# A different order of matmuls and loads in the first phase of a one-core transformer-layer kernel

## The chip, the cores and the metric

The kernel runs on one core of a Trainium2 chip. TensorE does the matmuls, VectorE (DVE in the profile) and ScalarE (ACT) the elementwise work, GpSimd (POOL) a little of it, and SyncE (SP) issues nearly all loads from HBM. The metric is the device time of one execution in microseconds; lower is better.

## The reference

One layer over 256 latent tokens `x` and 256 context tokens `ctx`, each 2048 wide, in float32. What the first phase computes is this part:

```python
mod   = silu(c) @ w_mod + b_mod          # one row of 6*2048; sa, ca, ga, sm, cm, gm are its six pieces
mod_c = silu(c_ctx) @ w_mod + b_mod      # the same for the context's conditioning vector
h_c = rmsnorm(ctx, w) * (1 + ca_c) + sa_c
h   = rmsnorm(x,   w) * (1 + ca)   + sa
k_c = rmsnorm(split(h_c @ w_k));  q, k = rope(rmsnorm(split(h @ w_q))), rope(rmsnorm(split(h @ w_k)))
```

After it come the values, the rest of the queries and keys, attention, a pooling mixer, gates, an output projection and a squared-ReLU MLP. A change in the first phase leaves all of these as they are.

## The kernel before, in words

Every product of float32 operands is made of three matmuls: each operand is split in a high part (rounded) and a low part (the remainder), and high·high, low·high and high·low are added up in PSUM (`mm3`). A weight chunk of 128x1024 (512 KB) is loaded to a `raw` buffer by SP; ACT copies it rounded to a `whi` tile and DVE subtracts to get `wlo` (in `load_next`, the lines 232 and 233). The order of all loads is written down ahead of time: `plan(...)` appends to the list `stream`, and `wchunk` takes the next chunk, after `load_next` has issued the loads up to `ahead` chunks further on. SP issues in the order of that list and waits at a load whose buffer isn't free yet.

The contraction over the 2048 model channels is cut in 16 tiles of 128 channels. The first phase loops over these tiles, `f` = 0 to 15. For each one:

- `mod_tile(f)` uses four `w_m` chunks (2 MB) in 32 small matmuls (the `mod` tile in the profile) to get shift and scale of that tile's channels, for latents and context at once. `mod_columns` turns the result into columns with four tiny matmuls (`modT`) and a few short ACT and DVE instructions.
- `hidden(f, 0)` and `hidden(f, 1)` make the modulated, normalised latents (`hL`) and context tokens (`hC`) of the tile: two DVE instructions and one ACT instruction each. They need the factor `rms`, which comes from sums of squares over all channels (`ssq`); for the context that sum is made by `context_squares` from the four `cT` loads.
- The first halves of keys and queries (512 of 1024 columns) are accumulated tile by tile: `kx` (keys of latents), `q` (queries of latents), `kc` (keys of context), six matmuls of 128x512 each. The weights come in pairs of tiles: chunk `j` of `w_k` and of `w_q` holds the tiles 2j and 2j+1.

All matmuls of this phase stay in the order in which the program gives them (`ordered_pe`); ACT's and DVE's instructions are put in an order by the compiler's scheduler. Products are taken from one chain (`order`, `side`) at a pace written in a table: `PACE[f]` half-products are done around `mod_columns`, so tile 0's keys are first multiplied at `f` = 2, and the chain then trails the modulation by about two tiles. The two chunks of the last pair are multiplied after the loop, with the rest of the chain.

Buffers matter for the order. The `raw` tag has five buffers of 512 KB; the `w_m` chunks of even tiles and all `w_k`, `w_q` chunks use them. The `w_m` chunks of odd tiles use other memory (`mod_raw`, lines 179 to 187). An even tile and one pair of `w_k` and `w_q` thus are six chunks for five buffers. In the kernel before, the pair is loaded behind the odd tile (`f` = 1, 3, 7, 9, ...), except for the third, which comes right behind tile 6:

```python
j = 2 if f == 6 else -1 if f == 5 or f % 2 == 0 else f // 2
```

The high and low parts of `w_k` lie in a tile `first` with room for two chunks, those of `w_q` in the common `whi` and `wlo` tiles. SP's load is in the lines 115 (`w_k`, `w_q` and all later weights) and 212 (`w_m`). The next phase begins with the values, `v_group(0)`, whose matmuls are on the lines 426, 427 and 429; the profile gives line 67 for every matmul that is kept in program order.

Beside all this a background generator (`late_gen`) loads the remaining pieces of `w_mod` and sums them on DVE (line 606), at a rate tied to the weight chunks loaded. It starts after the first phase; chunks loaded earlier give it no step.

Of the kernel before, what the change touches and what calls it, by code (L numbers as in the profile page):

```python
# [19 lines left out]
KT = D // P  # L20
# [28 lines left out]
def layer(ctx: ExitStack, tc, a, out):  # L49
# [21 lines left out]
    def bank(name):  # L71
        return psum.tile([P, 512], F32, tag="ps", name=name)

    def work(name, shape=None, dt=F32):
        return pool.tile(shape or [P, 512], dt, tag="w2", name=name, bufs=9)

    def s16(name, shape, dt=F32):
        return pool.tile(shape, dt, tag="s16", name=name, bufs=7)
# [4 lines left out]
    def small(name, n):  # L83
        return pool.tile([P, 16], F32, tag="sm", name=name, bufs=12)[:, 0:n]
# [14 lines left out]
    def tick():  # L99
        for w in waiting:  # L100
            w[0] -= 1
        while waiting:
            due = [w for w in waiting if w[0] <= 0]
            if not due:
                break
            waiting.remove(due[0])
            due[0][1]()
# [10 lines left out]
    def chain(*gens):  # L118
        for g in gens:
            yield from g  # L120
# [5 lines left out]
    def plan(name, *idx, rate=0.0):  # L126
        stream.append(((name,) + idx, rate))
# [3 lines left out]
    for f in range(KT):  # L131
        for i in range(4):
            plan("w_m", f, i)
            if f in (2, 3) and i % 2 == 1:
                plan("cT", 2 * f - 4 + i // 2)
            if (f, i) == (9, 0):
                plan("prq")
        j = 2 if f == 6 else -1 if f == 5 or f % 2 == 0 else f // 2
        if j >= 0:
            plan("w_k", 0, j)  # L140
            plan("w_q", 0, j)
    for n, g, rate in (("w_v", 0, 1.5), ("w_q", 1, 1.0), ("w_k", 1, 1.5), ("w_v", 1, 1.5)):
        for ch in range(8):
            plan(n, g, ch, rate=rate)
# [27 lines left out]
    FIRST_AHEAD = 3  # L172
# [69 lines left out]
    def wchunk(*key, ahead=AHEAD):  # L242
        while len(loaded) < min(done[0] + 1 + ahead, len(stream)) or loaded[done[0]][1] is None:
            if loaded and done[0] < len(loaded) and loaded[done[0]][1] is None:
                done[0] += 1
                continue
            load_next()
        got, hi, lo = loaded[done[0]]
        assert got == key, (got, key)
        loaded[done[0]] = None  # L250
        done[0] += 1
        tick()
        return hi, lo
# [5 lines left out]
    def mm3(o, l_hi, l_lo, r_hi, r_lo, start, stop):  # L259
        pe.matmul(o, l_hi, r_hi, start=start, stop=False)  # L260
        pe.matmul(o, l_hi, r_lo, start=False, stop=False)
        pe.matmul(o, l_lo, r_hi, start=False, stop=stop)

    def rsq(v, n, div, tag=None):

        mk = (lambda nm: small(nm, n)) if n <= 16 else (lambda nm: work(nm, [P, n]))
        y = mk(tag or "rq_y")
        pin(act.activation(y, v, AF.Ln, scale=div * 2.0 ** -64, bias=epsb))
        act.activation(y, y, AF.Exp, scale=-0.5, bias=ebias)
        t = mk("rq_t")  # L270
        vec.scalar_tensor_tensor(t, y, -0.5 * div, y, ALU.mult, ALU.mult)
        vec.scalar_tensor_tensor(t, v, EPS / div, t, ALU.add, ALU.mult)
        vec.scalar_tensor_tensor(y, t, 1.5, y, ALU.add, ALU.mult)
        return y
# [6 lines left out]
    cT = s16("cT", [P, KT, T])  # L281
# [3 lines left out]
    def pr(name):  # L285
        lo, hi = PRM[name]
        return prm[:, lo:hi]
# [70 lines left out]
    def tok(tiles, k, part, t):  # L358
        return tiles[k // 8][:, part, k % 8, t * P:t * P + P]

    def mod_tile(f, ps):

        raws = [wchunk("w_m", f, i, ahead=FIRST_AHEAD)[0] for i in range(4)]
        c = (f % 2) * T
        for i in range(4):
            for j in range(4):
                k = 4 * i + j  # L370
                pe.matmul(ps[32 * j:32 * j + 32, c:c + T], cv[:, k, :], raws[i][:, j * T:j * T + T],
                          start=k < 4, stop=k >= 12)
        rows = work("rows", [P, T])
        act.copy(rows, ps[:, c:c + T])
        return rows

    def mod_columns(f, rows):

        pt = bank("modT")
        for a in range(2):  # L380
            pe.matmul(pt[:, 2 * a:2 * a + 2], rows[:, a * P:a * P + P], quads, start=a == 0, stop=a == 1,
                      skip_group_check=True)
        col = small("col", 4)
        act.copy(col, pt[:, 0:4])
        c3 = col.rearrange("p (a c) -> p a c", a=2)
        vec.tensor_add(c3, c3, bias2[:, :, f:f + 1].broadcast_to([P, 2, 2]))
        vec.tensor_scalar(c3[:, 0, :], c3[:, 0, :], pr("nw")[:, f:f + 1], None, ALU.mult)
        return c3

    def hidden(f, t, c3):  # L390

        src, h = ((xT, hL), (cT, hC))[t]
        u = work("hw", [P, T])
        ht, k8 = h[f // 8], f % 8
        bias = c3[:, 1, t:t + 1]
        vec.scalar_tensor_tensor(u, src[:, f, :], c3[:, 0, t:t + 1], rms[t], ALU.mult, ALU.mult)
        act.activation(ht[:, 0, k8, :], u, AF.Identity, bias=bias)
        vec.scalar_tensor_tensor(ht[:, 1, k8, :], u, bias, ht[:, 0, k8, :].bitcast(F32), ALU.add, ALU.subtract)

    def tokens(nt):  # L400
        return [(hL, 0), (hL, 1), (hC, 0), (hC, 1)][:nt]

    def xmm(banks, toks, k, hi, lo, sl, first, last):
        for ps, (h, t) in zip(banks, toks):
            mm3(ps, tok(h, k, 0, t), tok(h, k, 1, t), hi[:, sl], lo[:, sl], first, last)
# [72 lines left out]
    fb = {}  # L478
    held = {}

    def pair_steps(n, j):

        w = "w_q" if n == "q" else "w_k"
        if w not in fb:
            fb[w] = [bank(f"{w}_{t}") for t in range(4 if n != "q" else 2)]
        hi, lo = held[w, j]
        for kk in range(2):
            k = 2 * j + kk
            for t in range(2):
                t4 = t + (2 if n == "kc" else 0)  # L490
                xmm([fb[w][t4]], [tokens(4)[t4]], k, hi, lo, slice(kk * 512, kk * 512 + 512), k == 0, k == KT - 1)
                yield

    def steps(n):
        for _ in range(n):
            next(side, None)

    order = [("kx", 0), ("q", 0), ("kx", 1), ("q", 1), ("kc", 0), ("kc", 1), ("kx", 2), ("q", 2), ("kc", 2)]
    for j in range(3, 7):
        order += [("kx", j), ("q", j), ("kc", j)]  # L500
    side = chain(*(pair_steps(*o) for o in order))
    PACE = (0, 0, 4, 4, 6, 6, 8, 8) + (6,) * 8

    cols = {}
    total = []

    def context_squares(i):

        sq = [work("sq") for _ in range(2)]
        for h in range(2):  # L510
            act.activation(sq[h], cT[:, 4 * i + 2 * h:4 * i + 2 * h + 2, :].rearrange("p a t -> p (a t)"), AF.Square)
        vec.tensor_add(sq[0], sq[0], sq[1])
        if total:
            vec.tensor_add(total[0], total[0], sq[0])
        else:
            total.append(sq[0])


    context = {4: (0, 1), 5: (2, 3, 4), 6: (5, 6)}
    ordered_pe[0] = True  # L520
    sb = bank("ssq")
    for i in range(4):
# [2 lines left out]
    for f in range(KT):  # L525
        if f % 2 == 0:
            ps = bank("mod")
        rows = mod_tile(f, ps)
        if f == 4:
            sq = total[0]  # L530
            vec.tensor_add(sq[:, 0:T], sq[:, 0:T], sq[:, T:2 * T])
            sb = bank("ssq")
            pe.matmul(sb[:, 0:T], mean, sq[:, 0:T], start=True, stop=True)
            rms.append(rsq(sb[:, 0:T], T, P / D, "rms"))
        j = 2 if f == 6 else -1 if f == 5 or f % 2 == 0 else f // 2
        if j >= 0:
            for w in ("w_k", "w_q"):
                held[w, j] = wchunk(w, 0, j, ahead=FIRST_AHEAD if j < 7 else 1)
        steps(PACE[f] // 2)
        cols[f] = mod_columns(f, rows)  # L540
        steps(PACE[f] - PACE[f] // 2)
        hidden(f, 0, cols[f])
        for k in context.get(f, (f,) if f > 6 else ()):
            hidden(k, 1, cols[k])
        if f in (2, 3):
            for i in range(2):
                context_squares(2 * f - 4 + i)
        if f == 10:
            tables()
    lasts = [pair_steps(n, 7) for n in ("kx", "q", "kc")]  # L550
    for _ in range(2):
        for g in lasts:
            next(g)
            next(g)
    ordered_pe[0] = False
    kb, qb = fb["w_k"], fb["w_q"]
    qT = s8("qT", [P, NH, T])
# [592 lines left out]
```

## Time and profile before

| | |
|---|---|
| median of 3 runs | 1488.44 us (1488.24 to 1490.8) |
| the profiled execution | 1489.0 us |
| its span, first to last instruction | 1487.2 us |
| TensorE busy | 1452.3 us, 98% |
| VectorE busy | 993.1 us, 67% |
| ScalarE busy | 695.2 us, 47% |
| loaded from HBM | 344 MB, mean 233 GB/s |
| mean granted TensorE clock | 0.99 |

A busy share is the time in which at least one instruction of the engine was running. The chain of waits follows the execution back from its last instruction, at each step to what released it. Times in views with a window count from the first instruction. The first phase ends where the first matmul of `v` starts, at 144.8 us.

### The profile page before, as it was taken

The page shows a single profiled execution, that of the slowest core. Times are in us where ns is not written, and L with a number is a line of the kernel's source. Part 1 is how long each engine was busy: PE and PEld are TensorE (multiplying, and loading weights), DVE is VectorE, ACT ScalarE, POOL GpSimd, SP SyncE. Part 2 cuts the span into 40 slices and gives each one's busy share as a digit, 9 for nine tenths or more (in the row PEclk, how much of TensorE's full clock was granted, in tenths as well). Part 3 has the DMA queues.
Part 4 walks back from the last instruction along what each step waited for, and adds up shares of the span by engine and source line. Part 5 has one row for each costly group of instructions (what it writes and reads, how often), then busy time and mean ns, then how long its engine had stood idle before and what let it go on. Part 6 is the DMA issues. An engine that isn't in the chain of part 4 may idle for free.

```text
span 1487.2 us, 19656 instructions
## 1 busy us (share of the span) xinstructions
PE 1452.3 (98%) x7402; PEld 1192.0 (80%) x7402; DVE 993.1 (67%) x1227; ACT 695.2 (47%) x961; POOL 122.3 (8%) x120
## 2 busy tenths in 40 slices
PE   6899999999899999999989999999999999999998
PEld 3567887778888888888878888888888888888887
DVE  3555988859887676767676765666665555555675
ACT  4334344555654444444444554535445453544532
POOL 0000101101410000000000100100000000000260
PEclk7999999999999999999999999999999999999999
DMA  9898696456678887887756777777776666666564
GB/s 357 312 380 321 198 326 213 144 182 205 200 251 269 273 269 257 264 306 265 228 169 207 231 230 242 223 236 238 238 237 213 196 186 195 188 191 191 186 197 142
DMA packets 97439, 347.83 MB, mean 234 GB/s; under 512 B 11072, under 2 KB 11712, under 8 KB 97344
## 3 DMA queue, kind: packets, MB, share of 16 engines
q1 hardware_dynamic: 96768, 345.50, 70.5%
q8 instruction: 58, 0.95, 0.3%
q0 software_dynamic: 576, 1.08, 0.2%
q14 instruction: 37, 0.30, 0.1%
HBM read 344.44 MB, written 2.10 MB: 233 GB/s over the span
## 4 chain that ended last, share of the span: by engine, by line
PE 89%; DMA 5%; DVE 3%; ACT 1%; issue 1%; POOL 0%; SPq 0%; DVEq 0%; POOLq 0%; ACTq 0%
PE f L999 14%; PE f L427 8%; PE f L426 8%; PE f L429 8%; PE f L1002 7%; PE pg L426 4%; PE pg L427 4%; PE pg L429 4%; DMA raw<-in_w_m_dram 3%; PE pyy L426 2%; PE pyy L427 2%; PE pyy L429 2%; PE wo L427 2%; PE wo L426 2%; PE wo L429 2%; PE w_k L67 2%
## 5 line engine op out<-in xcount | busy, mean ns | idle before, releaser
L233 DVE TENSOR_TENSOR wlo<-raw,whi 128x1024 fp32r<-128x1024 f32 x441 | 546.3, 1240 | 351.6 <-ACT whi L232 329.0
L232 ACT CAST whi<-raw 128x1024 fp32r<-128x1024 f32 x441 | 461.7, 1048 | 563.9 <-PE f L427 184.9
L999 PE MATMUL f<-h,whi 128*128 128x512 f32 x896 | 224.3, 392 | 0.0
L427 PE MATMUL f<-whi,act 128*128 128x512 f32 x512 | 199.3, 389 | 0.0
L426 PE MATMUL f<-whi,act 128*128 128x512 f32 x512 | 199.3, 389 | 0.0
L999 PEld LDWEIGHTS f<-h,whi 128*128 128x128 f32 x896 | 161.7, 189 | 29.4
L606 DVE SCALAR_TENSOR_TENSOR macc<-raw,sil,macc 128x1024 f32<-128x1024 f32 x128 | 167.7, 1310 | 1.4 <-DMA macc<-in_b_cm_dram 0.9
L429 PE MATMUL f<-wlo,act 128*128 128x512 f32 x512 | 136.8, 389 | 0.0
L1002 PEld LDWEIGHTS f<-h,wlo 128*128 128x128 f32 x896 | 122.2, 190 | 8.7
L1002 PE MATMUL f<-h,wlo 128*128 128x256 f32 x896 | 124.9, 282 | 0.0
L429 PEld LDWEIGHTS f<-wlo,act 128*128 128x128 f32 x512 | 96.1, 188 | 19.9
L427 PEld LDWEIGHTS f<-whi,act 128*128 128x128 f32 x512 | 96.2, 188 | 19.8
L426 PEld LDWEIGHTS f<-whi,act 128*128 128x128 f32 x512 | 96.1, 188 | 19.8
L426 PE MATMUL pg<-whi,hL 128*128 128x512 f32 x256 | 100.7, 393 | 0.0
L427 PE MATMUL pg<-whi,hL 128*128 128x512 f32 x256 | 99.7, 389 | 0.0
L1010 POOL TENSOR_TENSOR rsq<-relu 128x512 f32<-128x512 f32 x28 | 29.1, 1040 | 538.5 <-ACT relu L1009 508.1
L429 PE MATMUL pg<-wlo,hL 128*128 128x512 f32 x256 | 68.5, 389 | 0.0
L426 PEld LDWEIGHTS pg<-whi,hL 128*128 128x128 f32 x256 | 48.1, 188 | 10.2 <-issue 0.2
L427 PEld LDWEIGHTS pg<-whi,hL 128*128 128x128 f32 x256 | 48.1, 188 | 10.1 <-issue 0.2
L429 PEld LDWEIGHTS pg<-wlo,hL 128*128 128x128 f32 x256 | 48.1, 188 | 10.1
L67 PE MATMUL mod<-raw,cv 128*32 128x256 f32 x512 | 38.4, 416 | 12.7 <-DMA raw<-in_w_m_dram 12.6
L426 PE MATMUL wo<-whi,mix 128*128 128x512 f32 x116 | 45.2, 390 | 0.0
(272 smaller groups left out, 2055.3 us busy)
## 6 DMA issues: line engine op xcount, KB each, us to landing
raw<-in_w_ff_dram SPq DMA_DIRECT2D x240, 512.0 KB, 4.3
raw<-in_w_m_dram SPq DMA_DIRECT2D x64, 512.0 KB, 8.2
raw<-in_w_ga_dram SPq DMA_DIRECT2D x32, 512.0 KB, 4.5
raw<-in_w_cm_dram SPq DMA_DIRECT2D x32, 512.0 KB, 4.5
raw<-in_w_gb_in_dram SPq DMA_DIRECT2D x32, 512.0 KB, 4.4
raw<-in_w_ga_in_dram SPq DMA_DIRECT2D x32, 512.0 KB, 4.6
raw<-in_w_sm_dram SPq DMA_DIRECT2D x32, 512.0 KB, 4.9
raw<-in_w_o_dram SPq DMA_DIRECT2D x32, 512.0 KB, 4.5
```

Source lines behind the costliest of these rows:

```text
L67: return (lambda *a, **k: pin(emit(*a, **k))) if self.flag[0] else emit
L232: act.copy(hi, raw)
L233: vec.tensor_sub(lo, raw, hi.bitcast(F32))
L426: pe.matmul(banks[t], tok(h, k, 0, tt), wt, start=k == 0, stop=False)
L427: pe.matmul(banks[t], tok(h, k, 1, tt), wt, start=False, stop=False)
L429: pe.matmul(banks[t], tok(h, k, 0, tt), wt, start=False, stop=k == 2 * nk - 1)
L606: pin(vec.scalar_tensor_tensor(acc, raw, sil[:, 0, k:k + 1], acc, ALU.mult, ALU.add))
L999: pe.matmul(ps, hi[:, kk * P:kk * P + P], both(h2, k), start=k == 0, stop=False)
L1002: pe.matmul(ps[:, T:2 * T], lo[:, kk * P:kk * P + P], act_slice(h2, k, 0), start=False, stop=k == KT - 1)
L1010: gp.tensor_mul(sq, r, r)
```

## The change

The four `cT` loads are put together behind tile 1. Chunk pair `j` is loaded behind the even tile 2j, for all j. The chain with its pace table is gone: `products(n, k)` does all six matmuls of one tile at once. For `f` of 3 and above the products of tile `f - 1` stand around the modulation of tile `f`; tiles 0 and 1 of the latents are multiplied right after their own modulation, and the context's first two tiles after the context's norm, which is now made at `f` = 2 with the context tiles 0 to 2 behind it. The loop's last loads are taken with a look-ahead of three chunks, where the last pair had one.

```diff
-            if f in (2, 3) and i % 2 == 1:
-                plan("cT", 2 * f - 4 + i // 2)
...
-        j = 2 if f == 6 else -1 if f == 5 or f % 2 == 0 else f // 2
-        if j >= 0:
-            plan("w_k", 0, j)
-            plan("w_q", 0, j)
+        if f % 2 == 0:
+            plan("w_k", 0, f // 2)
+            plan("w_q", 0, f // 2)
+        if f == 1:
+            for i in range(4):
+                plan("cT", i)
...
+    def products(n, k):
...
+        hi, lo = held[w, k // 2]
+        c = (k % 2) * 512
+        for t in range(2):
+            t4 = t + (2 if n == "kc" else 0)
+            xmm([fb[w][t4]], [tokens(4)[t4]], k, hi, lo, slice(c, c + 512), k == 0, k == KT - 1)
...
-    side = chain(*(pair_steps(*o) for o in order))
-    PACE = (0, 0, 4, 4, 6, 6, 8, 8) + (6,) * 8
...
+    def modulate(f, rows):
+        cols[f] = mod_columns(f, rows)
+        hidden(f, 0, cols[f])
+        if f > 2:
+            hidden(f, 1, cols[f])
...
         rows = mod_tile(f, ps)
...
+        if f % 2 == 0:
+            for w in ("w_k", "w_q"):
+                held[w, f // 2] = wchunk(w, 0, f // 2, ahead=FIRST_AHEAD)
+        if f == 0:
+            modulate(f, rows)
+            products("kx", 0)
+            products("q", 0)
+        elif f == 1:
+            modulate(f, rows)
+            products("kx", 1)
+            products("q", 1)
+        elif f == 2:
+            for i in range(4):
+                context_squares(i)
             sq = total[0]
             vec.tensor_add(sq[:, 0:T], sq[:, 0:T], sq[:, T:2 * T])
+            modulate(f, rows)
             sb = bank("ssq")
             pe.matmul(sb[:, 0:T], mean, sq[:, 0:T], start=True, stop=True)
             rms.append(rsq(sb[:, 0:T], T, P / D, "rms"))
...
+            for k in range(3):
+                hidden(k, 1, cols[k])
+            products("kc", 0)
+            products("kc", 1)
+        else:
+            products("kx", f - 1)
+            modulate(f, rows)
+            products("q", f - 1)
+            products("kc", f - 1)
...
+    for n in ("kx", "q", "kc"):
+        products(n, KT - 1)
```

More of the change, by code (lines that the diff above doesn't have):

```diff
@@ L479, in layer @@
     held = {}
-    def pair_steps(n, j):
+    def products(n, k):
         w = "w_q" if n == "q" else "w_k"
@@ L485, in pair_steps @@
             fb[w] = [bank(f"{w}_{t}") for t in range(4 if n != "q" else 2)]
[L486 to L500, printed above, removed]
-    side = chain(*(pair_steps(*o) for o in order))
-    PACE = (0, 0, 4, 4, 6, 6, 8, 8) + (6,) * 8
+        hi, lo = held[w, k // 2]
[3 more added lines that the diff above has]
+            xmm([fb[w][t4]], [tokens(4)[t4]], k, hi, lo, slice(c, c + 512), k == 0, k == KT - 1)
     cols = {}
@@ L516, in context_squares @@
             total.append(sq[0])
-    context = {4: (0, 1), 5: (2, 3, 4), 6: (5, 6)}
+    def modulate(f, rows):
[3 more added lines that the diff above has]
+            hidden(f, 1, cols[f])
     ordered_pe[0] = True
@@ L528, in layer @@
         rows = mod_tile(f, ps)
-        if f == 4:
+        if f % 2 == 0:
[12 more added lines that the diff above has]
+                context_squares(i)
             sq = total[0]
             vec.tensor_add(sq[:, 0:T], sq[:, 0:T], sq[:, T:2 * T])
+            modulate(f, rows)
             sb = bank("ssq")
@@ L534, in layer @@
             rms.append(rsq(sb[:, 0:T], T, P / D, "rms"))
[L535 to L547, printed above, removed]
+            for k in range(3):
[7 more added lines that the diff above has]
+            products("kc", f - 1)
         if f == 10:
             tables()
[L550 to L554, printed above, removed]
+    for n in ("kx", "q", "kc"):
+        products(n, KT - 1)
     ordered_pe[0] = False
```

## The prediction

> **What bounds the kernel now.** I read the page's busy times first, then the waits of TensorE before and after the first phase, then the chain of waits and the queue of loads inside that phase. The page says that TensorE is busy nearly always; the waits of TensorE from 144 us to the end say the same more sharply (columns: total us, times, longest):
>
> ```profile
> PE 1452.3 (98%) x7402; PEld 1192.0 (80%) x7402; DVE 993.1 (67%) x1227; ACT 695.2 (47%) x961; POOL 122.3 (8%) x120
> ```
> ```profile
> PE pin L262 <- DVE wlo L233: 4.1, 2, 2.3
> ```
>
> This is the longest of its waits in 1343 us. So whatever the first phase gains or loses moves the end by as much: nothing behind it has room to absorb a shift. The first phase itself is another matter. In it TensorE waits on `w_m`, and the loads run at their top rate (columns from the eighth: granted clock, DMA share, GB/s):
>
> ```profile
> PE mod L67 <- DMA raw<-in_w_m_dram: 12.6, 18, 2.2
> ```
> ```profile
> 12.00:16.00 4.00, 2.94 (x36) 1.13 (x35) 1.28 (x3) 1.33 (x3) 0.00 (x0) 1.00 1.02 410
> 44.00:48.00 4.00, 1.59 (x24) 0.32 (x16) 4.00 (x5) 2.33 (x4) 0.00 (x0) 1.00 0.62 198
> 48.00:52.00 4.00, 3.03 (x13) 1.85 (x14) 1.12 (x3) 1.10 (x3) 0.00 (x0) 0.50 1.03 420
> 60.00:64.00 4.00, 4.00 (x21) 3.12 (x19) 1.68 (x6) 0.87 (x3) 0.00 (x0) 1.00 0.03 8
> ```
> ```profile
> raw<-in_w_m_dram SPq DMA_DIRECT2D x64, 512.0 KB, 8.2
> ```
>
> At 410 GB/s a chunk of 512 KB (524,288 bytes) takes 1.28 us. A pair of tiles needs eight `w_m` chunks, one `w_k` and one `w_q`: ten chunks, 12.8 us. The chain of waits gives TensorE's side of it and how long a pair takes now:
>
> ```profile
> 97.00 0.64 PE mod L67 x8
> 97.64 2.27 PE w_k L67 x9
> 99.91 0.34 PE modT L67 x4
> ...
> 101.04 1.36 PE w_q L67 x6
> 102.40 1.86 PE mod L67 x32
> ...
> 106.94 3.95 DMA raw<-in_w_m_dram
> 110.89 0.04 issue
> 110.93 0.64 PE mod L67 x8
> ...
> 124.45 0.64 PE mod L67 x8
> ```
>
> Six products cost 1.36 us, so a tile costs 1.86 + 0.34 + 3 x 1.36 = 6.3 us of TensorE, a pair 12.6. Two resources are nearly level, and a pair takes 13.9 us (97.00 to 110.93) and 13.5 us (to 124.45), mean 13.7: 0.9 over the loads' 12.8. So the first phase is set by how well loads and matmuls overlap, that is by when SP may issue.
>
> The row of 60 to 64 us is the key. The load engines stand still there, with TensorE busy all the time. SP's waits name the cause, and TensorE's timeline and the load's own row show its course:
>
> ```profile
> SPq L115 <- PE mod L67: 8.1, 1, 8.1
> ```
> ```profile
> 64.04 1.93 PE L67 MATMUL mod<-raw,cv 128*32 128x256 f32 x32
> ```
> ```profile
> L115 SPq DMA_DIRECT2D raw<-in_w_q_dram x1: 328/328/328, 64.7 to 64.7; - x1
> ...
> DMA to landing us min/median/max: 3.7/3.7/3.7
> ```
>
> This is the one place in the kernel before where a `w_k`, `w_q` pair stands right behind an even tile's four chunks. These six need five buffers, so `w_q` waits for the even tile's first chunk to be used: TensorE began that tile at 64.04, and 0.7 us later (8 of its 32 matmuls) the load was issued, at 64.7. It then took 3.7 us to land, with nothing ahead of it in flight, and the odd tile's chunks, whose own buffers may long be free, stood behind it on SP.
>
> **The change part by part.** No operation is removed or added: 16 tiles with 18 products each, the same 32 calls of `hidden`, eight squares, and the same 88 chunks of 512 KB and one smaller load. Only the order changes. Four terms follow, in microseconds against the profiled execution.
>
> *Pairs 3 to 7: the loop through `w_q`.* Every pair now has the pattern of 50 to 68 us. Count from the landing of an odd tile's last chunk. TensorE does that chunk's 8 matmuls (0.64), then `kx` of the tile before, `modT`, `q` and `kc` (3 x 1.36 + 0.34 = 4.42), and only then the next even tile's first chunk (0.70); SP issues `w_q`, which lands 3.7 later, and four odd chunks follow at 1.28 each (5.12). One turn is 0.64 + 4.42 + 0.70 + 3.7 + 5.12 = 14.6 us against 12.8 by bandwidth. What is late next is the whole odd tile, since its chunks queue behind `w_q`, and with it TensorE, which runs out of chunks for about 2 us a turn. If `w_q` were issued 1.8 us earlier, nothing would be lost: that is the point from which this decides. On the 0.9 us that a pair now loses beyond bandwidth: a part comes from an even chunk that waits for the split of `w_k` and goes away, since six chunks stand between them now; the rest are stretches of slower loading that stay. I take half, so 15.0 a turn against 13.7, +1.3; bounds 14.6 - 13.7 = +0.9, and with all of the 0.9 and a landing of 4.0, as the chunk issued at 106.94 had, 15.8 - 13.7 = +2.1. Five pairs: **+6.5 (4.5 to 10.5)**.
>
> The Trainium skill, "DMA: Bandwidth & Descriptors", section "Anatomy of one DMA", fits the time of a load as 2.0 us plus its bytes over 436 GB/s (there for loads from GpSimd), an estimate of 3.2 us for a chunk where the row has 3.7. With 3.2 the turn would be 0.5 us shorter and this term 2.5 us smaller; I go by the row.
>
> *The head, up to 68.4 us.* There the third `w_q` lands in the kernel before (64.7 + 3.7) as the 42nd chunk: 4 of `xT`, 28 of `w_m`, 4 of `cT`, 6 of `w_k` and `w_q`. For the kernel after I follow TensorE, whose order is fixed. The rows:
>
> ```profile
> 14.94 0.64 PE L67 MATMUL mod<-raw,cv 128*32 128x256 f32 x8 [0.64 <-DMA raw<-in_w_m_dram]
> ...
> 30.53 2.93 PE L67 MATMUL w_k<-first,hL 128*128 128x512 f32 x6
> ...
> 49.98 1.22 PE L67 MATMUL ssq<-sq,mean 128*128 128x256 f32 x2
> ```
> ```profile
> 18.57 0.48 DVE L398 SCALAR_TENSOR_TENSOR hL<-hw,col,hL 128x256 fp32r<-128x256 f32 x1 [0.64 <-ACT hL L397]
> ...
> 53.20 0.43 DVE L273 SCALAR_TENSOR_TENSOR rms<-rq_t,rms 128x256 f32<-128x256 f32 x1
> ```
>
> From the end of a tile's modulation (15.58) to its `hL` (19.05) it is 3.5 us; at half clock six products take up to 2.93, so some 0.47 each; from `ssq` to the factor 53.63 - 49.98 = 3.7; a `hidden` is three instructions like the `hL` row's 0.48, 1.4 together. Tile 0's products now wait for their own `hL`: start 19.3, twelve at half clock, 25; tile 1's modulation (1.9), 26.9; its `hL` 30.4; twelve products at a clock between half and full (4.2), 34.6; tile 2, 36.5. `modT` and the start of `ssq` 1.0, the norm 3.7, context `hidden` 1.4: 42.6. TensorE has idled, so twelve more at half clock, 48.2; tile 3 50.1; its eighteen products and `modT` 54.5; tile 4's first chunk 55.2, and the third `w_q` lands at 58.9 as chunk 34 (4 + 20 + 4 + 6). Up to 68.4 another 9.5 / 1.28 = 7.4 chunks land: 41.4 against 42, **+0.8**. The squares of the context are counted as done before tile 2's modulation, on an ACT that waits there. If the scheduler puts them behind it, eight at 0.6 and their sums come on the path, 6.5 us more; if `hL` and norm come sooner by a third, 3 us less. ACT's price:
>
> ```profile
> 35.86 1.65 ACT L511 ACTIVATE sq<-cT 128x512 f32<-128x512 f32 x3
> ```
>
> *Two chunks moved ahead of tile 15.* The last pair used to land behind the last `w_m` chunk; now it is ahead of it: 2 x 1.28 = **+2.6**, whatever else happens.
>
> *The tail.* This is the gain:
>
> ```profile
> 129.85 2.04 PE mod L67 x32
> ...
> 144.81 0.23 PE v L426
> ```
>
> From the end of the last modulation (131.89) to the values it is 12.9 us, 54 products and a `modT`. Now 36 products are left: 6 x 1.36 + 0.34 = 8.5, and 0.2 of waiting for the last context `hidden`, which has only 4.1 us of products to hide in beside the first splits of `w_v`. 8.7 - 12.9 = **-4.2** (-3.2 to -4.4).
>
> Edits that I cost at nothing: the longer look-ahead loads two more chunks of `w_v` before the background sums can start, so three of their steps of 1.3 us of DVE move later, into the output projection. They are hidden by TensorE's matmuls there, and the last of `sm` still comes some ten chunks before it is needed; without that cover it would be 3 x 1.3 = 3.9 us. The context's `hidden` calls merely swap places with others.
>
> ```profile
> L606 DVE SCALAR_TENSOR_TENSOR macc<-raw,sil,macc 128x1024 f32<-128x1024 f32 x128 | 167.7, 1310 | 1.4 <-DMA macc<-in_b_cm_dram 0.9
> ```
>
> Sum: 6.5 + 0.8 + 2.6 - 4.2 = +5.7, so 1489.0 + 5.7 = 1494.7 by the profiled execution, whose span is 1487.2 with 1.8 around it. The median of the runs shown, 1488.44, is 0.56 below it: about **1494**.
>
> **The rivals.** *SP is not held at `w_q`: faster.* The scheduler could put an odd tile's four loads ahead of `w_q`, since their buffers are free. It decides from the 1.8 us on that are lost now: then the loop isn't there, a pair costs 12.8 + 0.45 = 13.25, five pairs -2.3; the head loses its last wait, about 3 less: -2.2; with +2.6 - 4.2 it is -6, 1482.5. For it: ACT's order shows the scheduler moving work. Against it: all 90 loads of the first phase stand on SP in the planned order, the wait of 8.1 us included.
>
> *The clock falls in every pair.* In 44 to 48 us TensorE was busy 1.59 of 4 us, and the next stretch ran at clock 0.50. A turn now has a stretch of about 3.3 us in which only an odd tile's chunks trickle in, 0.64 of matmul per 1.28. If the clock falls there, the 5.1 us behind it stretch by some 3 us, and each turn with them: 5 x 3 = 15, so 1509. Against it: half busy is more than 1.59 of 4.
> The Trainium skill, "TensorE: Matmul & The Clock Gate", section "HAM oscillation", has this very failure: a wait for a load in each turn of a loop, longer than a window of some 3.4 us, lets the clock drop again each turn. By it the idle pieces here, under 1 us each, are too short.
>
> *The context's squares are late*: +6.5, 1500.5. *The gaps are made up*: a landing 0.5 sooner and slow stretches that fall into the stops give pairs of 14.1, five times +0.4, with a head 3 shorter: 2.0 - 2.2 + 2.6 - 4.2 = -1.8, 1486.6.
>
> **How the numbers follow.** The likeliest, slower by about 6, gets 0.60; its own range by the bounds above (head -3 to +3) is 1489 to 1503. Late squares 0.09, the falling clock 0.07, made up 0.11, the faster one 0.13. From no change this kernel's times can tell about 0.2%, 3 us. Slower by more: 0.56 of the first, and the two slower rivals, 0.72; within: 0.13; faster: 0.15, with a little from shorter heads. For 8 in 10 I go from 1485 to 1503.
>
> **What would show it.** Right: at most pairs SP waits on `mod` before a `w_q` of line 115, that load lands some 3.7 us after its issue, and between the last waits of two even tiles lie about 15 us; `mod` waits for `w_m` more than 12.6 us in all; the values start near 150.5; behind that the traces differ by a constant. Wrong: loads without stops from 70 us on, or values before 145. A head that ends past 62 us at the third `w_q`, or clock 0.50 behind 60 us, would keep the sign but break the size.

## The result and the profile after

The changed kernel takes 1498.07 us (median of 4 runs, 1496.28 to 1499.74), the kernel before beside it 1488.34 us (1486.93 to 1490.8). The ratio is **1.0064, 95% interval 1.0051 to 1.0076**: slower by 9.7 us. The forecast was 1494, slower, with a range that holds the time; the sign and the main mechanism stand, one term was too small, and one came out right for a different reason.

The profiled execution after took 1499.74 us with a span of 1498.0, which is 10.8 longer than before. The busy times of the kernel after are nearly those of before (PE 1452.3, DVE 993.1, ACT 695.2), with the same 7402 matmuls: the change adds no work, only time without work.

```profile
span 1498.0 us, 19653 instructions
PE 1451.3 (97%) x7402; PEld 1193.9 (80%) x7402; DVE 992.8 (66%) x1227; ACT 694.9 (46%) x961; POOL 126.8 (8%) x120
```

The chain of waits of the kernel after, from 112 to 150 us (start, us, what), shows the turns of the loop and the tail.

```profile
112.27 0.64 PE mod L67 x8
112.91 1.58 PE w_k L67 x6
114.50 0.34 PE modT L67 x4
114.84 1.48 PE w_q L67 x6
116.31 1.36 PE w_k L67 x6
117.67 0.61 PE mod L67 x8
...
118.30 0.33 SPq L115
...
120.10 8.02 DMA raw<-in_w_m_dram
...
128.16 0.64 PE mod L67 x8
...
143.61 0.64 PE mod L67 x8
144.25 1.58 PE w_k L67 x6
...
149.06 0.23 PE v L426
```

Each turn is the loop that the prediction describes: last chunk of an odd tile, three times six products with `modT` between, eight matmuls of the next even tile, and only then SP issues the load of line 115, `w_q`. From that row on the chain runs through the loads to the next odd tile's last chunk, up to 8 us in which TensorE isn't the cause. The last two turns take 15.9 us (112.27 to 128.16) and 15.5 (to 143.61). Before, the pairs of the same chain took 13.9 and 13.5.

What the load queue does meanwhile stands in the waits of SP between 62 and 150 us of the kernel after, and in the loads between 118 and 123 us (KB each, us from issue to landing).

```profile
SPq L115 <- PE mod L67: 23.7, 5, 5.3
```
```profile
raw<-in_w_q_dram SPq DMA_DIRECT2D x1, 512.0 KB, 4.0
```

Five times SP stands at a load of line 115 until TensorE has used a chunk: 23.7 us in all, where the kernel before had 9.0, of which one wait is 8.1. The windows of the kernel after (length, the busy time of PE, PEld, DVE, ACT and POOL, then clock, DMA share, GB/s) show what that does: loads at 161 GB/s while TensorE works without a break, then loads at 413 GB/s while TensorE is busy 4.6 of 6 us.

```profile
102.00:106.00 4.00, 4.00 (x44) 2.75 (x44) 0.58 (x1) 1.36 (x3) 0.00 (x0) 1.00 0.54 161
106.00:112.00 6.00, 4.60 (x36) 2.41 (x35) 4.70 (x13) 2.40 (x5) 0.00 (x0) 1.00 1.02 413
```

The waits of TensorE up to 158 us in the kernel after hold a second surprise.

```profile
PE ssq L67 <- DVE sq L538: 8.4, 1, 8.4
PE mod L67 <- DMA raw<-in_w_m_dram: 7.5, 14, 0.8
```

`mod` waits less for `w_m` than before (12.6), although the phase is longer. The largest wait is now that of the sum of squares of the context, 8.4 us: its squares came late.

### The profile page after: what moved, and what is told of

It reads as the page before. It is cut to its first block, busy times and chain, and to the rows that moved or that the text cites. A ratio compares the mean times of both kernels' runs of the same rounds, so it can differ in the third digit from the quotient of the medians.

```text
span 1498.0 us, 19653 instructions
## 1 busy us (share of the span) xinstructions
PE 1451.3 (97%) x7402; PEld 1193.9 (80%) x7402; DVE 992.8 (66%) x1227; ACT 694.9 (46%) x961; POOL 126.8 (8%) x120
## 3 DMA queue, kind: packets, MB, share of 16 engines
q0 software_dynamic: 576, 1.08, 0.2%
## 4 chain that ended last, share of the span: by engine, by line
PE 88%; DVE 4%; DMA 4%; ACT 2%; issue 1%; POOL 1%; SPq 1%; DVEq 0%; POOLq 0%; ACTq 0%
PE f L1000 14%; PE f L427 8%; PE f L426 8%; PE f L429 8%; PE f L1003 7%; PE pg L427 4%; PE pg L426 4%; PE pg L429 4%; DMA raw<-in_w_m_dram 3%; PE w_k L67 2%; PE pyy L426 2%; PE pyy L427 2%; PE pyy L429 2%; PE wo L427 2%; PE wo L426 2%; PE wo L429 2%
## 5 line engine op out<-in xcount | busy, mean ns | idle before, releaser
L426 PE MATMUL wo<-whi,mix 128*128 128x512 f32 x116 | 45.3, 390 | 0.0
L427 PE MATMUL wo<-whi,mix 128*128 128x512 f32 x116 | 45.2, 389 | 0.0
```

The source lines that it names most:

```text
L426: pe.matmul(banks[t], tok(h, k, 0, tt), wt, start=k == 0, stop=False)
L427: pe.matmul(banks[t], tok(h, k, 1, tt), wt, start=False, stop=False)
```

## The experiments

Two limits were in question. One is the load order: an even tile and a pair need six places, the `raw` tag has five, and `w_q` waits. The other is the later norm of the context, with nothing for TensorE to do meanwhile. Each ratio below is against the kernel before on the same chip.

**A buffer of its own for `w_q`, in the kernel after.** The raw chunk of `w_q` goes to the buffers of the tag `wlo`, so that the even tile's four chunks and `w_k` have the five `raw` buffers to themselves.

```diff
-        raw = raw_chunk(src, n)
+        if key[:2] == ("w_q", 0):
+            raw = pool.tile([P, n], F32, tag="wlo", name="raw", bufs=3)
+            sp.dma_start(raw, src)
+        else:
+            raw = raw_chunk(src, n)
```

> The changed kernel, with the first phase's w_q chunks loaded to a buffer of their own (the third one of the wlo tag, idle in this phase) instead of the five raw buffers; nothing is left out. Theory (the loop through w_q): SP no longer waits for an even tile's matmuls before w_q, so a pair of tiles takes about 13.3 us instead of 15.3, the last modulation ends some 10 us earlier (near 134 us against 144.3), and the time falls by about 10 us, to 1488. Rival (TensorE's own chains of modulation, hidden and norm set the pace): SP's wait goes, but the pairs stay near 15 us and the time at 1496 or more.

Measured: 1490.22 us (1488.76 to 1491.82), ratio 1.000 (0.9989 to 1.0011). That is 7.9 us under the kernel after, or 9.5 by the two ratios, which each go against the kernel before timed beside it. The waits of TensorE up to 140 us in this kernel:

```profile
PE ssq L67 <- DVE sq L542: 8.4, 1, 8.4
PE mod L67 <- DMA raw<-in_w_m_dram: 0.4, 1, 0.4
```

The wait for `w_m` is nearly gone, and the last modulation ends at 134.29 in place of 144.25. From 53 to 134 us TensorE now works without a break, at 6.62 us a tile or 13.24 a pair (tile 12's modulation starts at 112.50, tile 14's at 125.74). The loads keep up, at 12.8 us a pair in the last turns, which is what the bytes of ten chunks take at 410 GB/s. With the loop gone TensorE is the limit, so the loop through `w_q` carried the loss. The wait for the squares stays.

**The same buffer in the kernel before.** The same edit there, as a control: its one wait of 8.1 us goes too.

> The kernel before with w_q's own buffer and nothing else. It had one pair behind an even tile, the third, and a wait of 8.1 us on SP there. Theory: that wait goes, the stop of the loads at 60 to 66 us with it, and as far as TensorE isn't the bound by then the time falls by 2 to 5 us, to 1484 to 1487. Rival (TensorE had a backlog at 50 to 72 us, so the stop cost it nothing): no change, 1489.

Measured: 1482.84 us (1480.75 to 1485.36), ratio 0.9955 (0.9941 to 0.9969). In the windows of this kernel two stretches are full in which the kernel before loaded at 198 GB/s (44 to 48 us) and at 8 (60 to 64), and the clock doesn't fall to 0.50 at 48 us as it did there:

```profile
44.00:48.00 4.00, 1.55 (x17) 0.61 (x18) 3.51 (x6) 1.09 (x3) 0.00 (x0) 1.00 1.03 410
48.00:52.00 4.00, 4.00 (x21) 3.38 (x20) 2.17 (x7) 1.15 (x3) 0.00 (x0) 1.00 1.04 411
60.00:64.00 4.00, 4.00 (x40) 2.79 (x33) 2.67 (x5) 2.77 (x5) 0.00 (x0) 1.00 1.03 405
```

This changes how the first experiment is to be read. That the kernel after came back to the time of before doesn't mean that the loop is all that the change costs: the same want of buffers cost the kernel before 6.3 us itself (1489.1 to 1482.8). Not all of that belongs to the one stop at 60 us. In the traces the last modulation ends 8.2 us earlier (123.74 against 131.89). Tile 5's modulation, ahead of the stop, is already 4.5 earlier (52.88 against 57.42); tile 7's, behind it, ends 5.9 earlier; the rest comes at the later even tiles. With `w_q`'s own buffer in both, the rest of the change still costs 1490.2 - 1482.8 = 7.4 us (6.7 by the ratios).

**`w_q` between the odd tile's second and third chunk.** The other cure: no new buffer, but the blocked load stands behind two loads whose buffers are free.

```diff
+            if f % 2 == 1 and f > 1 and i == 1:
+                plan("w_q", 0, f // 2)
...
         if f % 2 == 0:
             plan("w_k", 0, f // 2)
-            plan("w_q", 0, f // 2)
+        if f == 0:
+            plan("w_q", 0, 0)
...
-        raws = [wchunk("w_m", f, i, ahead=FIRST_AHEAD)[0] for i in range(4)]
+        raws = []
+        for i in range(4):
+            if f % 2 == 1 and f > 1 and i == 2:
+                held["w_q", f // 2] = wchunk("w_q", 0, f // 2, ahead=FIRST_AHEAD)
+            raws.append(wchunk("w_m", f, i, ahead=FIRST_AHEAD)[0])
...
-            for w in ("w_k", "w_q"):
+            for w in ("w_k", "w_q") if f == 0 else ("w_k",):
```

> The changed kernel with w_q planned two odd chunks later, between the odd tile's second and third chunk, from the second pair on; buffers and all else as they are. Theory (the loop through w_q): SP can issue two odd chunks while TensorE gets to the even tile, so 2.6 us of loads cover the wait; turns fall from 15.3 to about 13.5, and the time by 6 to 9 us, to 1489 to 1492. Rival (the turn is set by TensorE's order, whatever SP does): 1497 to 1499.

Measured: 1491.0 us (1489.54 to 1493.19), ratio 1.001 (1.0002 to 1.0019). From the fifth landing of `w_q` on the turns take 12.8 to 13.8 us. The waits of SP between 62 and 150 us, and those of TensorE for `w_m`, in this kernel:

```profile
SPq L115 <- PE mod L67: 22.9, 5, 5.3
```
```profile
PE mod L67 <- DMA raw<-in_w_m_dram: 2.5, 4, 0.6
```

SP waits for `mod` as long as in the kernel after (23.7), and it costs next to nothing: two odd chunks are on their way during the wait. The length of a queue's wait says little; what stands behind it does.

**The pair loads alone, in the kernel before.** Only the place of the loads changes, the norm stays early. Some products of the keys read a later pair's `w_k` in this kernel, because its places are used again before they are done: the work is the same in kind and amount, the values are not the layer's.

```diff
-        j = 2 if f == 6 else -1 if f == 5 or f % 2 == 0 else f // 2
+        j = f // 2 if f % 2 == 0 else -1
```

> The kernel before, with one part of the change alone: every pair of w_k and w_q chunks is loaded behind the even tile; the context, the order of the products and the pace stay as before. Theory (the loop through w_q): pairs of 15 us again, +8 to +10 us, two more chunks ahead of the last modulation, +2.6, and no gain in the tail, since the products still trail: about 1499 to 1501, slower than the whole change. Rival (the loss comes from the products' order and the context's norm): near 1488 to 1491.

Measured: 1498.16 us (1495.07 to 1500.72), ratio 1.0051 (1.0036 to 1.0067). The chain of waits of this kernel, from 125 us on:

```profile
125.95 0.64 PE mod L67 x8
...
140.86 0.64 PE mod L67 x8
141.50 1.59 PE w_q L67 x6
...
154.42 0.23 PE v L426
```

The order of the loads alone makes the kernel as slow as the whole change does. Two expectations failed: it is not slower than the whole change, and its turns are not of 15 us. From the third landing of `w_q` (50.4 us, 11 earlier than in the kernel after) to the eighth (135.7) they take 17.1 on average; why was not followed, but one of them has a fall of the clock, at 95 us. Its last modulation ends at 141.50, 2.75 before that of the kernel after, and from there to the values it is 12.9 us: no gain in the tail. So the 4.2 us of the tail belong to the new order of the products, as the prediction has it.

**The context's squares earlier, in the kernel after.** The loads of the context are asked for and its squares issued behind tile 1's modulation, so that the norm no longer waits for them.

```diff
         elif f == 1:
             modulate(f, rows)
+            load_next()
+            for i in range(4):
+                context_squares(i)
...
         elif f == 2:
-            for i in range(4):
-                context_squares(i)
```

> The changed kernel, with the context's squares given to ACT and DVE at tile 1 instead of tile 2; the fourth context load is issued at the same place of SP's queue. Theory: TensorE's wait of 8.4 us before the context's ssq shrinks to under 2 us, the head gets some 6 us shorter, and as the turns behind it keep their length, the time falls by 5 to 6 us, to 1492. Rival (in the head the loads are the bound, and the squares are hidden behind them): under 2 us of gain.

Measured: 1502.31 us (1496.57 to 1506.52), ratio 1.0076 (1.0056 to 1.0095). This is no gain of some 5 us. Whether it is a loss against the kernel after (1.0064, 1.0051 to 1.0076) can't be told, as the intervals overlap. The rival had no gain either, but for a reason that doesn't hold, since the head did become shorter: tile 4's modulation starts at 55.0 us, 5 earlier. Then three turns take 17 to 20 us each. The windows of this kernel and its TensorE timeline say why.

```profile
72.00:80.00 8.00, 5.54 (x41) 2.83 (x45) 4.03 (x8) 2.24 (x4) 0.00 (x0) 0.89 0.99 356
80.00:84.00 4.00, 4.00 (x18) 2.66 (x10) 0.00 (x0) 0.37 (x1) 0.00 (x0) 0.50 1.01 411
```
```profile
73.42 1.52 PE L67 MATMUL w_k<-first,hC 128*128 128x512 f32 x6
75.56 0.64 PE L67 MATMUL mod<-raw,cv 128*32 128x256 f32 x8 [0.62 <-DMA raw<-in_w_m_dram]
77.06 0.64 PE L67 MATMUL mod<-raw,cv 128*32 128x256 f32 x8 [0.86 <-DMA raw<-in_w_m_dram]
78.36 1.08 PE L67 MATMUL mod<-raw,cv 128*32 128x256 f32 x8 [0.66 <-DMA raw<-in_w_m_dram]
```

Eight matmuls take 0.64 us and then, from 78.36 on, 1.08: the granted clock fell, and it stayed at 0.50 through 80 to 84 us. From 74.94 to 78.36 TensorE was busy for 2 x 0.64 = 1.28 of 3.42 us. The same thing happens from 99 and from 116 us on. The shorter head is paid back by longer turns, with 13.7 us at half clock in them.

**Filler in the odd tile.** To tell the clock from other causes, four matmuls into a bank that nothing reads follow each of the first three chunks of every odd tile from tile 5 on. They add work and take nothing away. First in the kernel with the early squares:

```diff
+    fill = bank("fill") if f % 2 == 1 and f > 3 else None
...
+        for j in range(4 if fill is not None and i < 3 else 0):
+            pe.matmul(fill[32*j:32*j+32, 0:T], cv[:, 4*i+j, :],
+                      raws[i][:, j*T:j*T+T], start=True, stop=True)
```

> The changed kernel with the early squares alone (median 1502.3), with four more matmuls behind each of the first three chunks of every odd tile from tile 5 on, written to a bank that nobody reads; they add work in TensorE's idle pieces and change no result. In that kernel the granted clock fell to 0.50 in three turns and a turn took 17 us. Theory (the idle pieces of the odd tile let the clock fall): no fall between 70 and 150 us, turns of 15 to 16 us, and 4 to 8 us less, 1494 to 1498, although there is more work. Rival (the clock's fall has another cause, or costs nothing): 1502 or more.

Measured: 1495.28 us (1492.01 to 1499.83), ratio 1.004 (1.0026 to 1.0054), 7 us faster with more work. The two intervals only just don't meet (1.0054 against 1.0056), since the runs of both kernels scatter by 8 to 10 us. The trace is clearer. The windows of this kernel:

```profile
80.00:84.00 4.00, 4.00 (x37) 2.69 (x39) 2.16 (x6) 0.97 (x3) 0.00 (x0) 1.00 0.58 230
60.00:150.00 90.00, 87.32 (x760) 59.20 (x760) 41.62 (x99) 31.09 (x63) 0.00 (x0) 1.00 0.86 330
```

The clock is 1.00 throughout where the same 90 us of the kernel without filler had 0.92. The fourth `w_q` lands level in both (72.2 and 72.5 us), the eighth 7.9 us earlier with filler (134.8 and 142.7). Not all of that is the clock: the filler also moved the fourth `w_q` behind one odd chunk in SP's order, and the last chunk of tile 7 lands 1.3 us earlier (78.44 against 79.72).

The same filler in the kernel after, whose clock didn't fall, is the control:

> The changed kernel as it is, with the same extra matmuls in the odd tiles from tile 5 on: the control of the run before, since here the clock did not fall in the turns. Theory (the extra matmuls helped there by the clock alone): no gain here, 1497 to 1500, or up to 2 us more where they delay TensorE. Rival (they help in another way, as by shifting the order of the loads): 1492 to 1495 here too.

Measured: 1497.34 us (1497.19 to 1502.53), ratio 1.0057 (1.0044 to 1.0071), against 1498.07: no difference, although here too the filler moved `w_q` one odd chunk back, in three pairs. So filler, and the order of the loads that comes with it, gains nothing where the clock doesn't fall; that it helped above mainly by the clock fits both runs.

**Both cures together, in the kernel after.** `w_q`'s own buffer and the early squares.

> The changed kernel with both edits, w_q's own buffer and the early squares. Theory: the two losses lie one behind the other, so the gains add: 10 + 6, about 1482, which is faster than the kernel before by 6 us. Rival (with one gone the other is hidden, as the loads are then the bound): 1486 to 1488, no better than the buffer alone.

Measured: 1482.82 us (1482.03 to 1484.83), ratio 0.9951 (0.9938 to 0.9964). Waits of TensorE up to 140 us in this kernel:

```profile
PE ssq L67 <- DVE sq L478: 7.5, 1, 7.5
PE w_k L67 <- ACT hC L401: 6.2, 1, 6.2
```

The first row is the start of the program, which every kernel here has. No wait for `w_m` is left in that list, and none for the context's squares. By the ratios the buffer alone brought 9.5 us, the squares alone nothing clear of noise, and both bring 16.8: with the loop in the way, the shorter head was lost again in the turns behind it, and with the loop gone it counts. Against the kernel before with its own buffer (1482.84) this is a draw, so the new order by itself has no lead left.

**Products in the wait of the norm.** The 6.2 us that are left there are filled with tile 2's products of keys and queries, which need only the latents.

```diff
         elif f == 2:
...
+            products("kx", 2)
+            products("q", 2)
             products("kc", 0)
...
-            products("kx", f - 1)
+            if f > 3:
+                products("kx", f - 1)
             modulate(f, rows)
-            products("q", f - 1)
+            if f > 3:
+                products("q", f - 1)
```

> The changed kernel with w_q's own buffer and the early squares (median 1482.8), and tile 2's keys and queries of the latents put into the wait for the context's norm, 6.2 us in which TensorE stood still, ahead of the context's keys. Theory: TensorE is now busy without a break from there to the end of the phase, so work put into the wait comes off the end: 12 products, 2.7 us at full clock, and 3 at most if the clock returns sooner: 1480. Rival: the products wait there for tile 2's hL and the w_q split, or run at half clock, and nothing is gained: 1482 to 1483.

Measured: 1479.13 us (median of five; four took 1478.2 to 1479.19, the fifth 7179, and why was not followed), ratio 0.9927 (0.9914 to 0.9940). It is 10 us below the kernel before and the fastest of all. The waits of TensorE up to 140 us:

```profile
PE mod L67 <- DMA raw<-in_w_m_dram: 1.1, 2, 0.6
```

The wait of 6.2 us on `hC` is no longer in the list; this one for `w_m` is new, and that for `hL` has grown from 3.8 to 5.1. The time fell by 3.7, where 2.7 to 3 were expected. In the traces the last modulation ends 5.1 us earlier (124.54 against 129.60), and 1.4 of it is lost again behind the first phase, where this trace has two falls of the clock and that of the kernel without these products one.

## Why the prediction was right, and where it was not

From the trace the difference of 10.8 us between the two spans divides so: +0.5 up to 68.4 us, +9.3 in the loop, +2.6 for the two chunks, -4.2 in the tail, +2.6 behind the first phase.

**The loop through `w_q`: right in kind, too small.** 15.0 us a turn were taken; from the third to the eighth landing of `w_q` it was 15.3 on average (61.3 to 138.0 us), and 15.5 to 15.9 in the last two turns. There the parts are 0.64 + 4.76 + 0.61 + 3.97 + 5.84 in place of 0.64 + 4.42 + 0.70 + 3.7 + 5.12. The mis-sized terms of the sum are three: products that take 4.76, since the eighteen cost 1.58, 1.48 and 1.36 by the chain and not 1.36 each; a landing of 4.0, the size that stood only in the upper bound; and four odd chunks that take 0.72 more than their bytes at 410 GB/s. TensorE's own part was too small in the same way: a pair costs it 13.24 us, as both kernels with `w_q`'s own buffer show, and not 12.6, so of the 0.9 us that a pair lost before only some 0.5 were waiting for loads. The step that failed is "I take half" of those 0.9 us: the slow stretches did not go away. Stops and slow stretches of the loads behind 68.4 us add up to 15.0 us, before to 5.7, which is the +9.3, between the 6.5 taken and the bound of 10.5.

**The head: right in its sum, wrong in its course.** 41.6 chunks have landed at 68.4 us (41.4 predicted, 42 before). But two errors cancel. "The squares of the context are counted as done before tile 2's modulation" is false: that was the rival of the late squares. The scheduler put ACT's squares behind the copy of tile 2's modulation, as ACT's timeline and then TensorE's, both of the kernel after, show.

```profile
34.94 0.37 ACT L374 COPY rows<-mod 128x256 f32<-128x256 f32 x1 [5.61 <-PE mod L67]
35.21 1.15 ACT L499 ACTIVATE sq<-cT 128x512 f32<-128x512 f32 x2
```
```profile
44.36 1.19 PE L67 MATMUL ssq<-sq,mean 128*128 128x256 f32 x2 [8.39 <-DVE sq L538]
49.09 4.40 PE L67 MATMUL w_k<-first,hC 128*128 128x512 f32 x12 [3.54 <-ACT hC L397]
53.42 1.93 PE L67 MATMUL mod<-raw,cv 128*32 128x256 f32 x32
```

Tile 3's modulation starts at 53.42, where the working had it end at 50.1. What made up for it is the first rival, in part: in the third, fourth and fifth pair SP's order has `w_q` behind three, two and one of the odd chunks. SP's timeline of the kernel after shows the third pair's, between two `w_m` chunks.

```profile
54.56 0.33 SPq L212 DMA_DIRECT2D raw<-in_w_m_dram  x1
55.86 0.33 SPq L115 DMA_DIRECT2D raw<-in_w_q_dram  x1
56.28 6.29 SPq L212 DMA_DIRECT2D raw<-in_w_m_dram  x6
```

It landed at 61.3 us as the 37th chunk, not at 58.9 as the 34th, and the loads ran on while TensorE waited. The argument against that rival, that SP keeps the planned order, held only for the kernel before. That `w_q` behind odd chunks does no harm is what the experiment with `w_q` between them shows. In the kernel with early squares SP put it right behind `w_k` again in the fourth and fifth pair, which may be part of its longer turns.

**Two chunks and the tail: right.** The two chunks are counted, at 1.28 us each: 88 land before the end of the modulations, 86 before the change. From the last modulation's end (144.25) to the end of the products it is 8.7 us, leaving out five matmuls of `v` that the scheduler pulled ahead of the last products; 12.9 before. By the chain the first `v` starts at 149.06, earlier than the 150.5 forecast, but for that reason alone: without the five the values would start near 153.0, 8.2 later than before.

**"Behind that the traces differ by a constant": not quite.** 1345.0 us lie behind 153.0, and 1342.4 behind 144.8 before. The windows of the kernel after, and then that of before, show places where the granted clock fell.

```profile
301.00:305.00 4.00, 4.00 (x12) 3.17 (x11) 1.35 (x2) 1.56 (x3) 1.46 (x2) 0.57 0.17 69
407.00:411.00 4.00, 4.00 (x23) 4.00 (x22) 3.93 (x10) 3.69 (x7) 0.14 (x2) 0.57 0.78 260
782.00:786.00 4.00, 3.52 (x8) 2.82 (x9) 3.90 (x9) 1.55 (x4) 0.00 (x0) 0.57 0.60 155
```
```profile
389.00:393.00 4.00, 4.00 (x24) 4.00 (x23) 1.93 (x3) 2.98 (x6) 3.52 (x6) 0.57 0.74 230
```

Three falls stand against one. Over the profiles of these kernels that stretch takes 1341.9 to 1342.8 us with one fall (the kernel before and five experiments), 1343.9 to 1344.6 with two, 1345.0 with three (the kernel after), and 1346.8 with four (the filler in the kernel after): about 1.2 us each. They come at the same three places in all these traces, some 147, 250 and 630 us behind the start of the values, where TensorE pauses (busy 1.40, 1.72 and 1.48 us of the 3.41 before the three falls of the kernel after); in the trace of before the clock held at the first and the last. The mean clock of single executions of the kernel before ranges from 0.988 to 0.994 on one chip, so the time at half clock changes from one to the next. For this reason these 2.6 us aren't put down to the change; whether the change makes the falls more frequent was not tested.

**What would show it.** SP's waits on `mod` and turns of 15 us came as listed. "`mod` waits for `w_m` more than 12.6 us in all" did not: it is 7.5, in 14 pieces of 0.8 at most where before had 18 of up to 2.2. TensorE's waiting moved to the squares (8.4).

**The falling clock** did not come in the kernel after, as its small chance said, but one edit away it did. The reason given against it, that half busy is more than 1.59 of 4, is borne out, but narrowly; that idle pieces under 1 us are too short is not. In every trace falls and returns of the clock lie multiples of 3.41 us apart. The windows show the 3.41 us before the first and the third fall of the kernel with the early squares and a stretch in which its clock held, and then the least busy stretch of the kernel after between 70 and 145 us:

```profile
74.86:78.27 3.41, 1.36 (x17) 0.32 (x16) 1.24 (x3) 0.51 (x1) 0.00 (x0) 1.00 0.99 380
112.41:115.82 3.41, 1.74 (x24) 0.32 (x16) 1.86 (x8) 0.71 (x2) 0.00 (x0) 1.00 1.02 413
129.47:132.88 3.41, 1.81 (x24) 0.36 (x23) 1.65 (x4) 0.51 (x1) 0.00 (x0) 1.00 1.00 401
```
```profile
140.81:144.22 3.41, 1.89 (x25) 0.51 (x25) 0.84 (x2) 0.51 (x1) 0.00 (x0) 1.00 1.03 416
```

With TensorE busy 1.36 and 1.74 us (40 and 51%) the clock fell, with 1.81 and 1.89 (53 and 55%) it held. So the kernel after came close to the falling clock.

## What to carry to other kernels

A load order that asks for one buffer more than there are puts compute into the loop of the loads: each turn then lasts as long as the landing, the matmuls that free the buffer and the loads queued behind, one after another. Count the buffers that a group of loads needs at once, and either give the blocked load its own or put loads with free buffers ahead of it.

Where two limits are stacked, taking one away can show nothing; test both together, and give the kernel before the same cure before a change is judged by what it loses.

## What was not expected of the hardware

The clock fell without a single long pause. In the kernel with the early squares the idle pieces before the first fall were 0.62, 0.86 and 0.66 us, and before its three falls TensorE was busy 40, 39 and 51% of 3.41 us; with filler in the pauses it didn't fall. The Trainium skill, "TensorE: Matmul & The Clock Gate", section "HAM oscillation", states the rule as no idle gaps over some 3.4 us. Here the measurement differs from it: gaps a quarter as long sufficed when they made up about half of such a stretch or more. All eleven traces together, cut at the times of their own clock records, put the limit near a half: 48 of the 49 falls came behind a stretch with TensorE busy at most 51% (the other, near the start of the program, 67%), and no stretch behind which the clock held was below 47%.
